# LayerNorm of a convolution branch, computed on token rows instead of by matmuls with a matrix of ones

## The chip, the cores and the metric

The kernel runs on one core of a Trainium2 chip. The metric is the device time of one execution in microseconds (us), as the median of several runs. The core has five engines that each run their own instruction list in order and wait for one another through semaphores: TensorE (PE, matmul; PEld is its weight load), VectorE (DVE), ScalarE (ACT), GpSimd (POOL) and SyncE (SP, which here issues the transfers).

## What is computed

The program is an encoder of two layers over 256 tokens of width 1024. Each layer is a SwiGLU block, a pair of mixers side by side (windowed attention and a convolution), a second SwiGLU block and a gated embedding. The change lies in the convolution mixer, and there in one step:

```python
def layer_norm(x, g, b, eps=1e-5):
    mu = jnp.mean(xf, axis=-1, keepdims=True)
    var = jnp.mean(jnp.square(xf - mu), axis=-1, keepdims=True)
    y = (xf - mu) * lax.rsqrt(var + eps)
    return y * g + b
...
c_val, c_gate = jnp.split(c, 2, axis=-1)
c = c_val * jax.nn.sigmoid(c_gate)
c = depthwise_conv(c, conv_w[i], conv_b[i])          # 31 taps
c = jax.nn.silu(layer_norm(c, conv_ln_g[i], conv_ln_b[i]))
y_conv = c @ w_conv_out[i]
g_attn, g_conv = jnp.split(jax.nn.sigmoid(g), 2, axis=-1)
h = h + (g_attn * y_attn + g_conv * y_conv) @ w_o[i]
```

The convolution has 512 channels, so for each of the 256 tokens a mean and a variance are taken over 512 values.

## The kernel before

Activations are kept with the channel on the 128 partitions and the token along the row: `y`, the convolution's result, is 128 x 4 x 256 (four groups of 128 channels, 256 tokens). Large weights are not used as they come. `Weights` loads a unit of 1 MB into one of four raw buffers (line 76, on SP's queue), ACT rounds it to a high part `w_hi` (line 100) and DVE forms the remainder `w_lo` (line 101); a product is then three matmuls, high x high, high x low and low x high (lines 311 to 313). A raw buffer is free for the next load once these two are through with it. The weights of the attention output and the convolution output are the exception: they are used as they are, in plain float32 (`raw_spec`, and `products` at line 847), and their buffers are free when the last matmul has read them.

The order of work on each engine is made by a scheduler that goes by priorities; products are put out in groups, and the evacuation of a group's PSUM tile is put out after the first product of the next one (`group`, `flush`). PSUM tiles of one bank (`mm_tile`) come from a pool of four.

In `mix`, the stage around the change runs so: the last gates are computed (`ps_g`); the attention output is formed in four groups, `attn_out` (tile `ps_ao`, line 847, 8 plain matmuls each), and between these groups stands the LayerNorm; then the convolution output in four groups (`conv_out`, tile `ps_co`, 32 plain matmuls), which multiplies by the gates and adds the attention's part (lines 908 and 909), and splits the sum into `ym_h` and `ym_l` (lines 444 and 445); then the output projection (`mix_out`, tile `ps_wo`), which needs both and the split weights w_o. The 31 taps of the convolution run on DVE (line 607) and end during the attention output.

The LayerNorm before has the channels on partitions, so a sum over channels is a sum over partitions, and it is taken on PE: `ln_mean` multiplies `y` by a 128 x 128 matrix of 1/512 (`ones_c`), which leaves the mean of each token in every partition (`ps_mu`, line 866). DVE subtracts it (line 868), ACT squares (line 871, `ysq`), `ln_scale` multiplies the squares by the same matrix (`ps_var`, line 876), ACT takes the root (line 364), DVE the reciprocal over 128 x 256 (line 366), DVE scales (line 880), and ACT applies gain, bias and Silu (line 881). `table` (line 379) has ACT load the table of Silu ahead of it.

Of the kernel before, what the change touches and what calls it, by code (L numbers as in the profile page):

```python
# [9 lines left out]
F32 = mybir.dt.float32  # L10
F32R = mybir.dt.float32r
AF = mybir.ActivationFunctionType
ALU = mybir.AluOpType
AX = mybir.AxisListType

P = 128
T = 256
# [7 lines left out]
CD = 512  # L25
KC = CD // P
# [112 lines left out]
def encoder_kernel(ctx: ExitStack, tc: tile.TileContext, a: dict, out: bass.AP):  # L139
    nc = tc.nc  # L140
    PS = bass.MemoryType.PSUM

    const = ctx.enter_context(tc.tile_pool(name="const", bufs=1))
# [3 lines left out]
    tmp = ctx.enter_context(tc.tile_pool(name="tmp", bufs=2))  # L147
# [4 lines left out]
    def mm_tile(name):  # L152
        return mmp.tile([P, 512], F32, name=name, tag="mm")
# [5 lines left out]
    ident = const.tile([P, P], F32, name="ident")  # L159
# [130 lines left out]

    ones_d = const.tile([P, P], F32, name="ones_d")
    nc.gpsimd.memset(ones_d, 1.0 / D)
    ones_c = const.tile([P, P], F32, name="ones_c")
    nc.gpsimd.memset(ones_c, 1.0 / CD)
    eps6 = const.tile([P, 1], F32, name="eps6")
    nc.gpsimd.memset(eps6, 1e-6)
    eps5 = const.tile([P, 1], F32, name="eps5")
    nc.gpsimd.memset(eps5, 1e-5)

    def pcol(name, l, k):  # L300
        c0, n = col[name]
        return par[:, c0 + l * n + k : c0 + l * n + k + 1]
# [59 lines left out]
    def rsqrt_of(ps, eps, name, **kw):  # L362
        sd = tmp.tile([P, T], F32, name="sd", bufs=1)
        nc.scalar.activation(out=sd, in_=ps, func=AF.Sqrt, bias=eps)
        r = tmp.tile([P, T], F32, name=name, **kw)
        nc.vector.reciprocal(out=r, in_=sd)
        return r
# [9 lines left out]
    def table(func):  # L377

        tc.keep_in_program_order(nc.scalar.preload_act_table(func))
# [59 lines left out]
    def bcast(r, n):  # L439
        return r.unsqueeze(1).broadcast_to([P, n, T])  # L440
# [9 lines left out]
    with tc.manual_schedule(engines={mybir.EngineType.Activation, mybir.EngineType.DVE}):  # L450
# [7 lines left out]
        for k in range(KD):  # L458
            xT[k] = (mm_tile if 2 <= k < 6 else at_tile)("ps_xt")[:, :T]
            for t in range(2):  # L460
# [5 lines left out]
                out=xl, in0=xT[k], scalar=gain, in1=xh.bitcast(F32), op0=ALU.mult, op1=ALU.subtract  # L466
# [122 lines left out]
    def mix(l, u, st, xn, stat):  # L589
        cw, kg, bias, sink = (late[n] for n in ("cw", "kg", "bias", "sink"))  # L590
        with tc.tile_pool(name="mix_pool", bufs=1) as mp:
# [3 lines left out]
            y = mp.tile([P, KC, T], F32, name="y")  # L595
# [236 lines left out]
            def squash(i):  # L832
                gs = g[:, i : i + 4, :]
                tc.keep_in_program_order(nc.scalar.activation(out=gs, in_=gs, func=AF.Sigmoid))
# [17 lines left out]
            def attn_out(f):  # L852
                ps = mm_tile("ps_ao")

                def evac():
                    gs = g[:, f : f + 2, :]
                    nc.vector.tensor_tensor(out=gs, in0=ps.rearrange("p (c t) -> p c t", c=2), in1=gs, op=ALU.mult)

                group([lambda: products(ps, o)], evac)

            ysq = mp.tile([P, KC, T], F32, name="ysq", tag="sqq")

            def ln_mean():
                ps = mm_tile("ps_mu")
                for i in range(KC):
                    nc.tensor.matmul(ps[:, :T], ones_c, y[:, i, :], start=i == 0, stop=i == KC - 1)
                for i in range(0, KC, 2):
                    nc.vector.tensor_tensor(
                        out=y[:, i : i + 2, :], in0=y[:, i : i + 2, :], in1=bcast(ps[:, :T], 2), op=ALU.subtract
                    )  # L870
                    nc.scalar.activation(out=ysq[:, i : i + 2, :], in_=y[:, i : i + 2, :], func=AF.Square)

            def ln_scale():
                ps = mm_tile("ps_var")
                for i in range(KC):
                    nc.tensor.matmul(ps[:, :T], ones_c, ysq[:, i, :], start=i == 0, stop=i == KC - 1)
                rs = rsqrt_of(ps[:, :T], eps5, "rs", bufs=1)
                table(AF.Silu)
                for i in range(KC):
                    nc.vector.tensor_tensor(out=y[:, i, :], in0=y[:, i, :], in1=rs, op=ALU.mult)  # L880
                    nc.scalar.activation(
                        out=y[:, i, :], in_=y[:, i, :], func=AF.Silu,
                        scale=pcol("conv_ln_g", l, i), bias=pcol("conv_ln_b", l, i),
                    )

            for i in range(KC):
                if i == 1:
                    ln_mean()
                if i == 2:
                    ln_scale()  # L890
                attn_out(2 * i)
                if i == 0:
                    squash(12)
# [126 lines left out]
    for l in range(L):  # L1020
        with tc.tile_pool(name="ffn1_pool", bufs=1) as hp:
            hooks = {1: lambda: late_loads(hp), 5: late_params, 6: lambda: late_tables(hp), 8: late_write, 12: late_bias} if l == 0 else {}
            xn, stat = new_x("xa", f"xm{l}"), Stat()
            ffn(hp, l, x_cur, st, "norm_mix", xn, stat, hooks)
        x_cur, st = xn, stat.finish(3, tokens=True)
        xn, stat = new_x("xa", f"xf{l}"), Stat()
        mix(l, x_cur, st, xn, stat)
        x_cur, st = xn, stat.finish(3)
        with tc.tile_pool(name="ffn2_pool", bufs=1) as hp:
            xe = (hp.tile([P, KD, T], F32R, name="xe_h"), hp.tile([P, KD, T], F32R, name="xe_l"))  # L1030
            stat = Stat()
            ffn(hp, l, x_cur, st, "norm_pe", xe, stat, {0: lambda: embed_load(l), 4: lambda: embed_input(hp)})
            x_cur, st = xe, stat.finish(4)
            xn, stat = (new_x("xa", f"xn{l}") if l + 1 < L else None), Stat()
            embed(l, x_cur, st, xn, stat)
            x_cur, st = xn, stat.finish(3)
# [39 lines left out]
```

## Time and profile before

| | |
|---|---|
| runs, us | 1176.48, 1177.25, 1177.78 (median 1177.25) |
| the profiled execution, us | 1176.52 |
| its span (first to last instruction), us | 1174.7 |
| granted TensorE clock, mean | 0.999 |
| busy: PE, DVE, ACT, POOL, us | 1156.8, 813.6, 614.2, 88.5 |
| HBM read, MB | 200.53 |

All times in the profile are from the span's start. PE's busy time counts matmuls that overlap in the pipeline, so the spacing from one to the next is read from rows that merge several: their length less the last one's duration, by their count less one. A row of the timeline is: start, length, engine, line, operation, output <- inputs, shape, count, and in brackets how long the engine had been idle and who ended that. A row of the groups is: line, engine, operation, tiles, shapes, count | busy us in all, mean ns of one | idle before. In rows of the waits three numbers follow: us in total, times, longest.

### The profile page before, as it was taken

To read this page: it belongs to the slowest core of one execution; us is meant where nothing else is said; L and a number is where in the kernel's file an instruction comes from. 1 tells how busy PE (TensorE), PEld (TensorE's weight loads), DVE (VectorE), ACT (ScalarE), POOL (GpSimd) and SP (SyncE) were. 2 spreads that over 40 slices of the span, in tenths; PEclk is the share of its full clock that TensorE was granted. 3 is DMA by queue.
4 is the path that set the end of the run, shared out by engine and by line. 5 is a ranking of instruction groups with operands and counts; after the bars stand their busy time and mean duration, and the time that the engine had idled before them with its cause. 6 is when DMAs were issued, how large, how long until landed. Compare 5 with 4: busy or idle time off the path is not lost.

```text
span 1174.7 us, 21809 instructions
## 1 busy us (share of the span) xinstructions
PE 1156.8 (98%) x9082; PEld 1121.5 (95%) x9082; DVE 813.6 (69%) x1214; ACT 614.2 (52%) x1033; POOL 88.5 (8%) x119
## 2 busy tenths in 40 slices
PE   7999999999999999999999999999999999999997
PEld 7999999998889999999999999999987999999997
DVE  5866656798667766656876666569976786666564
ACT  6644444676356544444664444457753564444443
POOL 3000001211002000001110000113000010000110
PEclk9999999999999999999999999999999999999999
DMA  8866556545074565556556464566522664654541
GB/s 252 265 229 209 167 178 200 179 147 141 2 249 161 189 200 175 171 165 214 188 166 204 156 205 152 170 213 193 145 72 68 219 224 159 201 168 144 192 144 37
DMA packets 195694, 202.99 MB, mean 173 GB/s; under 512 B 3731, under 2 KB 188899, under 8 KB 195596
## 3 DMA queue, kind: packets, MB, share of 16 engines
q1 hardware_dynamic: 195564, 201.60, 53.6%
q8 instruction: 71, 1.16, 0.4%
q14 instruction: 27, 0.22, 0.1%
q10 hardware_dynamic: 32, 0.01, 0.0%
HBM read 200.53 MB, written 1.06 MB: 172 GB/s over the span
## 4 chain that ended last, share of the span: by engine, by line
PE 96%; DVE 2%; DMA 1%; ACT 1%; issue 0%; SPq 0%; ACTq 0%
PE ps_gu L313 14%; PE ps_gu L311 14%; PE ps_gu L312 14%; PE ps_fo L313 7%; PE ps_fo L312 7%; PE ps_fo L311 7%; PE ps_g L311 3%; PE ps_g L313 3%; PE ps_g L312 3%; PE ps_co L847 2%; PE ps_s L755 1%; PE ps_c L311 1%; PE ps_pe L313 1%; PE ps_pe L312 1%; PE ps_pe L311 1%; PE ps_c L313 1%
## 5 line engine op out<-in xcount | busy, mean ns | idle before, releaser
L101 DVE TENSOR_TENSOR w_lo<-raw,w_hi 128x1024 fp32r<-128x1024 f32 (+1 forms) x368 | 440.9, 1202 | 241.5 <-ACT w_hi L100 237.4
L100 ACT CAST w_hi<-raw 128x1024 fp32r<-128x1024 f32 (+1 forms) x368 | 377.2, 1030 | 427.0 <-PE ps_gu L312 215.3
L313 PE MATMUL ps_fo<-h_hi,w_lo 128*128 128x256 f32 x704 | 198.6, 283 | 0.0
L312 PE MATMUL ps_fo<-h_lo,w_hi 128*128 128x256 f32 x704 | 198.6, 283 | 0.0
L311 PE MATMUL ps_fo<-h_hi,w_hi 128*128 128x256 f32 x704 | 198.6, 283 | 0.0
L313 PEld LDWEIGHTS ps_fo<-h_hi,w_lo 128*128 128x128 f32 x704 | 134.9, 192 | 0.0
L311 PEld LDWEIGHTS ps_fo<-h_hi,w_hi 128*128 128x128 f32 x704 | 134.9, 192 | 0.0
L312 PEld LDWEIGHTS ps_fo<-h_lo,w_hi 128*128 128x128 f32 x704 | 134.9, 192 | 0.0
L400 POOL TENSOR_TENSOR sq_acc<-sq_acc,sq 128x256 f32<-128x256 f32 x56 | 56.5, 1010 | 903.4 <-ACT sq L399 902.9
L311 PE MATMUL ps_gu<-x0h,w_hi 128*128 128x256 f32 x352 | 100.8, 286 | 2.1 <-ACT x L456 2.1
L607 DVE SCALAR_TENSOR_TENSOR y<-cpad,cw,y 128x256 f32<-128x256 f32 x240 | 101.1, 477 | 0.1
L313 PE MATMUL ps_gu<-x0h,w_lo 128*128 128x256 f32 x352 | 100.4, 285 | 0.2 <-DVE w_lo L101 0.2
L312 PE MATMUL ps_gu<-x0l,w_hi 128*128 128x256 f32 x352 | 100.2, 285 | 0.0
L311 PE MATMUL ps_gu<-xn0h,w_hi 128*128 128x256 f32 x352 | 99.8, 284 | 0.0
L312 PE MATMUL ps_gu<-xf0l,w_hi 128*128 128x256 f32 x352 | 99.8, 284 | 0.0
L312 PE MATMUL ps_gu<-xf1l,w_hi 128*128 128x256 f32 x352 | 99.8, 284 | 0.0
L311 PE MATMUL ps_gu<-xf0h,w_hi 128*128 128x256 f32 x352 | 99.7, 283 | 0.0
L311 PE MATMUL ps_gu<-xf1h,w_hi 128*128 128x256 f32 x352 | 99.7, 283 | 0.0
L313 PE MATMUL ps_gu<-xf0h,w_lo 128*128 128x256 f32 x352 | 99.6, 283 | 0.0
L313 PE MATMUL ps_gu<-xn0h,w_lo 128*128 128x256 f32 x352 | 99.6, 283 | 0.0
L312 PE MATMUL ps_gu<-xn0l,w_hi 128*128 128x256 f32 x352 | 99.6, 283 | 0.0
L313 PE MATMUL ps_gu<-xf1h,w_lo 128*128 128x256 f32 x352 | 99.6, 283 | 0.0
(222 smaller groups left out, 2718.6 us busy)
## 6 DMA issues: line engine op xcount, KB each, us to landing
raw<-in_w_ffn_in_dram SPq DMA_DIRECT2D x86, 1024.0 KB
raw<-in_w_in_dram SPq DMA_DIRECT2D x30, 1024.0 KB
raw<-in_w_ffn_out_dram SPq DMA_DIRECT2D x32, 896.0 KB
raw<-in_w_ffn_out_dram SPq DMA_DIRECT2D x16, 1024.0 KB
raw<-in_w_o_dram SPq DMA_DIRECT2D x8, 1024.0 KB
raw<-in_w_pe_gate_dram SPq DMA_DIRECT2D x8, 1024.0 KB
raw<-in_w_attn_out_dram SPq DMA_DIRECT2D x8, 512.0 KB
raw<-in_w_conv_out_dram SPq DMA_DIRECT2D x4, 1024.0 KB
```

What stands on the lines that cost most here:

```text
L100: nc.scalar.copy(out=hv[:, :, d0 : d0 + w], in_=src),
L101: nc.vector.tensor_tensor(out=lv[:, :, d0 : d0 + w], in0=src, in1=hv[:, :, d0 : d0 + w].bitcast(F32), op=ALU.subtract,),
L311: nc.tensor.matmul(ps, wh[:, k0 + k, cols], xh[:, kx, :], start=f, stop=False)
L312: nc.tensor.matmul(ps, wh[:, k0 + k, cols], xl[:, kx, :], start=False, stop=False)
L313: nc.tensor.matmul(ps, wl[:, k0 + k, cols], xh[:, kx, :], start=False, stop=e)
L400: nc.gpsimd.tensor_tensor(out=self.acc, in0=self.acc, in1=sq, op=ALU.add)
L607: nc.vector.scalar_tensor_tensor(out=y[:, i, :], in0=src, scalar=w, in1=y[:, i, :], op0=ALU.mult, op1=ALU.add)
L755: nc.tensor.matmul(ps[:, c, :], qT[v * HD : (v + 1) * HD, c, qb * P : (qb + 1) * P], kT[v * HD : (v + 1) * HD, :], start=True, stop=True,)
L847: nc.tensor.matmul(ps[:, c * T : (c + 1) * T], w[:, k, c * P : (c + 1) * P], x[:, k, :], start=k == 0, stop=k == KC - 1,)
```

## The change

The LayerNorm is computed with the token on the partition. `ln_by_token` transposes `y` on PE, 128 x 128 at a time, into two PSUM tiles `ps_yt` (one for each 128 tokens, with 512 channels along the row); DVE takes the statistics of each row with BN_STATS and BN_AGGR into `mv` (mean and variance of each token); ACT takes the root of the variances (128 x 2), DVE the reciprocal, and DVE writes the normalised rows to `yn`, one pass for each tile. `ln_by_channel` transposes `yn` back on PE into two tiles `ps_yc`, and ACT applies gain, bias and Silu out of PSUM into `y`. The matrix `ones_c` and its memset go. The first half stands where the mean stood (ahead of the second attention group), the second half ahead of the fourth group; before, the second half stood ahead of the third.

```diff
-    ones_c = const.tile([P, P], F32, name="ones_c")
-    nc.gpsimd.memset(ones_c, 1.0 / CD)
...
-            ysq = mp.tile([P, KC, T], F32, name="ysq", tag="sqq")
-            def ln_mean():
-                ps = mm_tile("ps_mu")
-                for i in range(KC):
-                    nc.tensor.matmul(ps[:, :T], ones_c, y[:, i, :], start=i == 0, stop=i == KC - 1)
+            yn = mp.tile([P, 2, CD], F32, name="yn", tag="sqq")
+            def ln_by_token():
+                mv = tmp.tile([P, 2, 2], F32, name="mv")
+                ps = []
+                for t in range(2):
+                    ps.append(mm_tile("ps_yt"))
+                    for i in range(KC):
+                        nc.tensor.transpose(ps[t][:, i * P : (i + 1) * P], y[:, i, t * P : (t + 1) * P], ident)
+                    six = tmp.tile([P, 6], F32, name="six")
+                    nc.vector.bn_stats(out=six, in_=ps[t])
+                    nc.vector.bn_aggr(out=mv[:, t, :], in_=six)
+                rs = tmp.tile([P, 2], F32, name="rs")
+                nc.scalar.activation(out=rs, in_=mv[:, :, 1], func=AF.Sqrt, bias=eps5)
+                nc.vector.reciprocal(out=rs, in_=rs)
+                table(AF.Silu)
+                for t in range(2):
+                    nc.vector.tensor_scalar(
+                        out=yn[:, t, :], in0=ps[t], scalar1=mv[:, t, 0:1], scalar2=rs[:, t : t + 1],
+                        op0=ALU.subtract, op1=ALU.mult,
+                    )
+            def ln_by_channel():
                 for i in range(0, KC, 2):
-                    nc.vector.tensor_tensor(
-                        out=y[:, i : i + 2, :], in0=y[:, i : i + 2, :], in1=bcast(ps[:, :T], 2), op=ALU.subtract
-                    )
-                    nc.scalar.activation(out=ysq[:, i : i + 2, :], in_=y[:, i : i + 2, :], func=AF.Square)
-            def ln_scale():
-                ps = mm_tile("ps_var")
-                for i in range(KC):
-                    nc.tensor.matmul(ps[:, :T], ones_c, ysq[:, i, :], start=i == 0, stop=i == KC - 1)
-                rs = rsqrt_of(ps[:, :T], eps5, "rs", bufs=1)
-                table(AF.Silu)
-                for i in range(KC):
-                    nc.vector.tensor_tensor(out=y[:, i, :], in0=y[:, i, :], in1=rs, op=ALU.mult)
-                    nc.scalar.activation(
-                        out=y[:, i, :], in_=y[:, i, :], func=AF.Silu,
-                        scale=pcol("conv_ln_g", l, i), bias=pcol("conv_ln_b", l, i),
-                    )
+                    ps = mm_tile("ps_yc").rearrange("p (f t) -> p f t", f=2)
+                    for f in range(2):
+                        for t in range(2):
+                            nc.tensor.transpose(
+                                ps[:, f, t * P : (t + 1) * P], yn[:, t, (i + f) * P : (i + f + 1) * P], ident
+                            )
+                    for f in range(2):
+                        nc.scalar.activation(
+                            out=y[:, i + f, :], in_=ps[:, f, :], func=AF.Silu,
+                            scale=pcol("conv_ln_g", l, i + f), bias=pcol("conv_ln_b", l, i + f),
+                        )
             for i in range(KC):
                 if i == 1:
-                    ln_mean()
-                if i == 2:
-                    ln_scale()
+                    ln_by_token()
+                if i == 3:
+                    ln_by_channel()
                 attn_out(2 * i)
```

The scheduler places the new instructions. On PE, in layer 0, from the first attention matmul to the first of the output projection, the order before is:

```order
L847 MATMUL ps_ao<-o,raw 128x256 x8
L866 MATMUL ps_mu<-y,ones_c 128x256 x2
L847 MATMUL ps_ao<-o,raw 128x256 x6
L866 MATMUL ps_mu<-y,ones_c 128x256
L847 MATMUL ps_ao<-o,raw 128x256 x2
L866 MATMUL ps_mu<-y,ones_c 128x256
L876 MATMUL ps_var<-ysq,ones_c 128x256 x2
L847 MATMUL ps_ao<-o,raw 128x256 x9
L876 MATMUL ps_var<-ysq,ones_c 128x256 x2
L847 MATMUL ps_ao<-o,raw 128x256 x7
L847 MATMUL ps_co<-y,raw 128x256 x32
L311 MATMUL ps_wo<-ym_h_3783,w_hi 128x256 x3
```

and in the changed kernel (its lines are 2 lower up to the LayerNorm and 9 higher behind it):

```order
L845 MATMUL ps_ao<-o,raw 128x256 x8
L867 MATMUL ps_yt<-ident,y 128x128 x4
L845 MATMUL ps_ao<-o,raw 128x256 x6
L867 MATMUL ps_yt<-ident,y 128x128 x2
L845 MATMUL ps_ao<-o,raw 128x256 x6
L867 MATMUL ps_yt<-ident,y 128x128 x2
L845 MATMUL ps_ao<-o,raw 128x256 x4
L886 MATMUL ps_yc<-ident,yn 128x128 x2
L845 MATMUL ps_ao<-o,raw 128x256 x8
L886 MATMUL ps_yc<-ident,yn 128x128 x6
L845 MATMUL ps_co<-y,raw 128x256 x32
L309 MATMUL ps_wo<-ym_h_3791,w_hi 128x256 x4
```

The sixteenth attention matmul, with which the first raw buffer comes free, had three mean matmuls ahead of it and now has six transposes. The first two transposes back stand ahead of the last eight attention matmuls, and the projection begins with four products of the high halves where it began with three.

On DVE, at the same place, from the last two taps to the first evacuation of the convolution output (`w_lo` is the split of the weights w_o), the order before is:

```order
L607 SCALAR_TENSOR_TENSOR y<-cpad,cw,y 128x256 x2
L857 TENSOR_TENSOR g<-ps_ao,g 128x512
L868 TENSOR_TENSOR y<-y,ps_mu 128x512 x2
L101 TENSOR_TENSOR w_lo<-raw,w_hi 128x1024 x2
L857 TENSOR_TENSOR g<-ps_ao,g 128x512
L366 RECIPROCAL rs<-sd 128x256
L880 TENSOR_TENSOR y<-y,rs 128x256 x4
L857 TENSOR_TENSOR g<-ps_ao,g 128x512
L101 TENSOR_TENSOR w_lo<-raw,w_hi 128x1024 x4
L908 TENSOR_TENSOR g<-ps_co,g 128x512
```

and in the changed kernel:

```order
L605 SCALAR_TENSOR_TENSOR y<-cpad,cw,y 128x256 x2
L855 TENSOR_TENSOR g<-ps_ao,g 128x512
L869 BN_STATS six<-ps_yt 128x6 x2
L870 BN_AGGR mv<-six 128x2 x2
L855 TENSOR_TENSOR g<-ps_ao,g 128x512
L873 RECIPROCAL rs<-rs 128x2
L876 TENSOR_SCALAR yn<-ps_yt,mv,rs 128x512 x2
L101 TENSOR_TENSOR w_lo<-raw,w_hi 128x1024 x2
L855 TENSOR_TENSOR g<-ps_ao,g 128x512
L101 TENSOR_TENSOR w_lo<-raw,w_hi 128x1024 x3
L917 TENSOR_TENSOR g<-ps_co,g 128x512
```

The first two splits, which stood ahead of the reciprocal, now stand behind the whole LayerNorm; and the third attention evacuation stands ahead of the small reciprocal.

On DVE again, from there to the first `ym_l`, which the projection waits for, before:

```order
L101 TENSOR_TENSOR w_lo<-raw,w_hi 128x1024 x4
L908 TENSOR_TENSOR g<-ps_co,g 128x512
L909 TENSOR_TENSOR g<-g 128x512
L101 TENSOR_TENSOR w_lo<-raw,w_hi 128x1024
L908 TENSOR_TENSOR g<-ps_co,g 128x512
L445 TENSOR_TENSOR ym_l_3784<-g,ym_h_3783 128x512
```

and in the changed kernel:

```order
L101 TENSOR_TENSOR w_lo<-raw,w_hi 128x1024 x3
L917 TENSOR_TENSOR g<-ps_co,g 128x512
L101 TENSOR_TENSOR w_lo<-raw,w_hi 128x1024
L918 TENSOR_TENSOR g<-g 128x512
L917 TENSOR_TENSOR g<-ps_co,g 128x512
L918 TENSOR_TENSOR g<-g 128x512
L917 TENSOR_TENSOR g<-ps_co,g 128x512
L101 TENSOR_TENSOR w_lo<-raw,w_hi 128x1024
L443 TENSOR_TENSOR ym_l_3792<-g,ym_h_3791 128x512
```

Two evacuations of the convolution output and two sums stand ahead of the fifth split where there was one of each, and none stands between that split and `ym_l`. The order of transfers on SP is the same in both kernels. On ACT the changed kernel rounds the weights w_o twice ahead of the four Silu and five times behind them. Layer 1 has the same order in each kernel.

## The prediction

> **What bounds the kernel now.** I read the page first, then the busy time by stretches, then who PE waited for, then the chain that ended last, and last the order of time around the projections behind the attention.
>
> ```profile
> span 1174.7 us, 21809 instructions
> PE 1156.8 (98%) x9082; PEld 1121.5 (95%) x9082; DVE 813.6 (69%) x1214; ACT 614.2 (52%) x1033; POOL 88.5 (8%) x119
> PE 96%; DVE 2%; DMA 1%; ACT 1%; issue 0%; SPq 0%; ACTq 0%
> ```
>
> PE is busy 98% of the span and is 96% of the chain that ended last. Time can only be won in two ways: less work on PE, or fewer of its few waits. The table by stretches shows where the LayerNorm stage lies in both layers, and that PE is not full there (columns: stretch, length, busy time of PE, PEld, DVE, ACT, POOL, granted clock, DMA).
>
> ```profile
> 313.50:334.00 20.50, 17.78 (x83) 15.01 (x82) 12.43 (x21) 8.00 (x10) 0.00 (x0) 1.00 0.27 88
> 334.00:348.00 14.00, 14.00 (x65) 12.35 (x66) 9.81 (x13) 6.95 (x9) 0.00 (x0) 1.00 0.88 287
> 889.60:910.00 20.40, 17.83 (x83) 15.06 (x82) 12.46 (x21) 8.03 (x10) 0.00 (x0) 1.00 0.29 91
> ```
>
> PE lacks 2.72 us in the first layer's stretch and 2.57 in the second's, at a full clock; the stretch behind it, 334 to 348, is full. The waits name the reason, and both are the LayerNorm's own:
>
> ```profile
> PE ps_var L876 <- ACT ysq L871: 3.2, 2, 1.6
> PE ps_co L847 <- ACT y L881: 2.1, 2, 1.1
> ```
>
> So per layer: 1.6 us for the squares ahead of the variance and 1.1 us for the first normalised channel ahead of the convolution output. The chain, in order of time, in layer 0:
>
> ```profile
> 313.71 3.46 PE ps_ao L847 x16
> 317.17 0.86 PE ps_mu L866 x4
> 321.95 5.09 DMA raw<-in_w_o_dram
> 327.06 1.05 ACT w_hi L100
> 328.14 2.36 DVE w_lo L101 x2
> 330.50 0.60 DVE g L857
> 331.10 1.67 DVE rs L366
> 333.31 0.61 ACT y L881
> 333.97 14.08 PE ps_co L847 x64
> ```
>
> A matmul of plain float32 shows as two records: 16 records in 3.46 us are 8 matmuls of 0.43 us. The reciprocal over 128x256 stands behind two splits of weights that had waited for a transfer.
>
> **The change, PE's work.** It takes away 8 matmuls per layer (four for the mean, four for the variance; 4 records take 0.86 us): 8 x 0.43 = 3.44 us. It adds 16 transposes. The trace has the same transposes, for the attention, eight in a row, and the duration of one by itself:
>
> ```profile
> 277.63 1.03 PE L792 MATMUL ps_pt<-ident,s 128*128 128x128 f32 x8
> L792 PE MATMUL ps_pt<-ident,s x64: 270/272/332, 272.6 to 877.6; 128*128 128x128 f32 x64
> ```
>
> Eight in 1.03 us with 0.27 for the last are (1.03 - 0.27) / 7 = 0.108 us from one to the next. 16 x 0.108 = 1.73 us, so PE's work falls by 1.71 us per layer.
>
> **The change, the chain that PE waits for.** What is added on DVE and ACT, by the nearest rows:
>
> ```profile
> L857 DVE TENSOR_TENSOR g<-ps_ao,g 128x512 f32<-128x512 f32 x8 | 5.5, 687 | 6.8 <-PE ps_ao L847 6.8
> L765 DVE CUSTOM_DVE_ANT_0 s<-ps_s,bias,sink 128x256 f32<-128x256 f32 x32 | 13.6, 479 | 5.9 <-PE ps_s L755 4.0 <-PE ps_pt L792 1.9
> L366 DVE RECIPROCAL rs<-sd 128x256 f32<-128x256 f32 x2 | 3.5, 1743 | 0.0
> L421 ACT ACTIVATE sd_tok<-ps_stat,eps x2: 255/256/257, 214.7 to 790.8; 128x4 f32<-128x4 f32 x2
> L423 DVE RECIPROCAL r_tok<-sd_tok x2: 120/120/120, 216.5 to 792.6; 128x4 f32<-128x4 f32 x2
> L379 ACT ACT_TABLE_LOAD x2 | 2.6, 1283 | 0.0
> L881 ACT ACTIVATE y<-y,par 128x256 f32<-128x256 f32 x8 | 4.4, 591 | 2.3 <-DVE y L880 2.3
> ```
>
> BN_STATS and BN_AGGR are in no row. From below: a pass over 512 elements out of PSUM takes 0.69 us (0.60 when the next follows). The dearest DVE operation per element is the reciprocal, 1743 / 256 = 6.8 ns, which for 512 would be 3.5 us. In between, a pass with a running reduction (L765) takes 479 ns for 256, no more than other passes of its size. BN_STATS is a streaming reduction, so I take 0.69 and keep 3.5 as the upper end. For BN_AGGR and the tiny reciprocal I take 0.13 (L423), for the root over 128x2 0.26 (L421), for the normalising pass 0.69. The root's table load runs early, as ACT is idle after the last sigmoid; the Silu table (1.28) is covered by the transposes.
>
> Now PE's row in the new order, from 313.71. Eight attention matmuls to 317.17, four transposes to 317.60, six matmuls to 320.20, two transposes to 320.42, two matmuls to 321.28, four to 323.01, the last two transposes to 323.23. Their input is there: the last taps of the convolution end before 319 (the row below). Then four matmuls to 324.96, and the first two transposes back must wait for the normalised row.
>
> ```profile
> 317.88 0.99 DVE L607 SCALAR_TENSOR_TENSOR y<-cpad,cw,y 128x256 f32<-128x256 f32 x2
> ```
>
> On DVE: two BN_STATS from 323.3 end at 324.6, two BN_AGGR at 324.9, the root on ACT at 325.2; the third attention group, which PE ends at 324.96, is evacuated first (the DVE order has it ahead of the reciprocal), to 325.85; reciprocal 326.0; first normalising pass 326.7. So PE stands from 324.96 to about 326.75: 1.8 us, with eight ready matmuls queued behind the wait. They follow to 330.43, six transposes to 331.08, and the first Silu (0.59) lets the convolution output start near 331.6 instead of 333.97, 2.35 earlier. As a sum: 1.71 less work, waits of 1.8 + 0.5 in place of 2.72; the 0.25 between 2.1 and 2.35 is in no row (313.71 + 13.84 + 3.44 + 2.72 also falls 0.26 short of 333.97). I take the step by step figure; the sum is within the range.
>
> **What is late next.** The output projection needs weights that come through the raw buffers, and its input's low half. These rows are that path:
>
> ```profile
> 330.53 0.37 SPq L76 DMA_DIRECT2D raw<-in_w_o_dram  x1
> 332.89 0.37 SPq L76 DMA_DIRECT2D raw<-in_w_o_dram  x1
> 335.59 1.99 ACT L100 CAST w_hi<-raw 128x1024 fp32r<-128x1024 f32 x2 [0.69 <-DMA raw<-in_w_o_dram]
> 336.66 2.36 DVE L101 TENSOR_TENSOR w_lo<-raw,w_hi 128x1024 fp32r<-128x1024 f32 x2 [1.84 <-ACT w_hi L100]
> 338.52 1.99 ACT L100 CAST w_hi<-raw 128x1024 fp32r<-128x1024 f32 x2 [0.44 <-DMA raw<-in_w_o_dram]
> 339.05 0.37 SPq L76 DMA_DIRECT2D raw<-in_w_o_dram  x1
> 343.96 1.04 ACT L100 CAST w_hi<-raw 128x1024 fp32r<-128x1024 f32 x1 [3.44 <-DMA raw<-in_w_o_dram]
> 344.91 0.61 ACT L444 CAST ym_h<-g 128x512 fp32r<-128x512 f32 x1
> 345.03 1.23 DVE L101 TENSOR_TENSOR w_lo<-raw,w_hi 128x1024 fp32r<-128x1024 f32 x1 [1.75 <-ACT w_hi L100]
> 346.78 0.68 DVE L445 TENSOR_TENSOR ym_l<-g,ym_h 128x512 fp32r<-128x512 f32 x1
> 348.23 0.28 PE L312 MATMUL ps_wo<-ym_l,w_hi 128*128 128x256 f32 x1
> ```
>
> Each transfer waits for a buffer: the first for the 16th attention matmul (321.95), the second for the splits of the first (330.50), the fourth for the splits of the second (339.02). ym_l ends at 347.46, and PE reaches it at 348.23: about 0.7 us of slack. This path doesn't move by 2.35. The 16th matmul comes 0.65 earlier, since six transposes (0.65) stand ahead of it in place of three mean matmuls (1.29); cast and splits follow as before (DVE is free at 327.4), so the second transfer's cast starts at 334.94 and the third's 2.93 later, at 337.87. From 339.0 DVE has a full queue in the new order: splits and gate passes of 1.13, 0.60, 1.13, 0.60, 0.60, 0.75, 0.60, 1.23 and ym_l with 0.69 end at 346.4. PE ends the convolution output at 331.6 + 13.84 = 345.44, does four products that need only the high half (0.12 each) to 345.9, and waits 0.6 for ym_l, until 346.5. That is 1.73 before 348.23, with one product (0.12) more behind it: **1.85 us per layer**. Behind that point the weights come earlier too (the SP queue's order is the same), and PE is full as before.
>
> **Sum.** Two layers (the second has the same rows and the same order): 3.7 us. The profiled execution took 1176.52, 1.8 over its span: 1172.8. The median of the runs, 1177.25, is 0.7 above that execution, so on it 1173.55, which I round to **1173.6**. The rest costs nothing: ones_c's memset ran on POOL at the start, where nothing waits for it, and yn takes the buffer of ysq.
>
> **Rivals.**
> *All of PE's gain is kept (0.11).* If the DVE queue from 339.0 is 0.6 shorter than I add up, ym_l is no wait: 2 x 2.35 = 4.7, 1172.5. Against it: every piece of that queue has a row.
> *The statistics cost more, in part (0.11).* Each us on the two BN_STATS together moves the normalised row, and nearly all of it shows, since PE and the splits both stand behind it. BN_STATS of 0.85 to 1.65 us gives 0 to 3.3 us of gain; at 1.2, 1.85 - 1.0 = 0.85 per layer, 1175.5.
> *The statistics turn it slower (0.07).* The point is 1.85 = 2 x (t - 0.69), t = 1.6 us for one BN_STATS. At the reciprocal's price of 3.5 each layer loses 2 x 2.8 - 1.85 = 3.8 us: 1184.8. For it: no row shows the instruction. Against it: row L765, a reduction at the price of a plain pass.
> *Transposes at their latency (0.04).* If each took the 272 ns of the single row, PE would do 16 x 0.164 = 2.6 us more and the start at 331.6 would become 334.2: 0.2 late per layer, 1177.7, no change. The row of eight in 1.03 us speaks against it. The Trainium skill, "TensorE: Matmul & The Clock Gate", Part 4: PE-mode transpose, gives about 275 ns for a transpose in a kernel, says that latency dominates it and that transposes don't count as busy for the clock. By it this change would save nothing; the trace agrees with the duration of one and not with its use as a spacing, and it shows a granted clock of 1.00 in the stretch.
> *The second and third weight transfers share the way (0.07).* They are issued 0.6 us apart now, not 2.36. If they shared it evenly, the second would land some 2.2 later, ym_l would end near 348.5, and each layer would lose about 0.9: 1179. Against it: 330.53 to 335.59 is 5.06 us with the third in flight for the last 2.7, while the first alone took 5.11 (321.95 to 327.06).
>
> **How the numbers follow.** A measurement of this kernel can tell about 0.2%, 2.35 us, from no change. My forecast has 0.60 (waits and hand-overs 0.4 off per layer either way). Faster by over 0.2%: 0.60 + 0.11 + 0.03 of the dearer statistics (below 1.0 us each) = 0.74. Slower by over 0.2%: 0.07 for the statistics and 0.02 of the shared way = 0.09. The rest, 0.17, is no change. The range: below to 1172.0, the full gain and 0.5; above to 1176.9, which takes in the dearer statistics nearly to their turning point; outside are about 2 in 10.
>
> **What would show it.** ps_yt and ps_yc transposes 0.11 us apart; PE idle for yn about 1.8 us and for y about 0.5; ps_co starting 2.35 earlier; a wait of 0.6 for ym_l ahead of ps_wo where there was none; BN_STATS near 0.69. I am wrong if BN_STATS takes over 1 us, if the wait for ym_l is absent or over 1.5 us, or if stretches far from this stage move.

## The result and the profile after

The changed kernel takes 1158.15 us (median of 4 runs, 1156.98 to 1158.72) against 1177.3 beside it: a ratio of 0.9837, interval 0.982 to 0.9854. That is 19 us, where 3.7 were forecast; the direction was right, and the time lies far outside the range. The page begins (span, busy times, the chain that ended last):

```profile
span 1155.2 us, 21808 instructions
PE 1137.2 (98%) x9082; PEld 1102.3 (95%) x9082; DVE 811.0 (70%) x1214; ACT 610.9 (53%) x1029; POOL 87.4 (8%) x118
PE 95%; DMA 3%; DVE 1%; ACT 1%; issue 0%; SPq 0%; ACTq 0%; DVEq 0%
```

PE has as many records as before (9082; in each layer 8 float32 matmuls, which are 16 records, went, and 16 transposes came) and is busy 19.6 us less, when the change alone takes some 3.4 of work off it. So first the stage itself. The stretches of the attention output and of the convolution output (columns as in the prediction's table):

```profile
309.80:328.00 18.20, 16.01 (x83) 13.60 (x82) 12.27 (x22) 6.56 (x8) 0.00 (x0) 1.00 0.20 63
328.00:342.20 14.20, 14.10 (x65) 12.10 (x65) 8.39 (x10) 6.95 (x10) 0.00 (x0) 1.00 0.90 290
```

Rows of PE's timeline there in layer 0 (those between them are left out), and then of DVE's:

```profile
309.87 3.62 PE L845 MATMUL ps_ao<-o,raw 128*128 128x256 f32 x16
313.32 0.60 PE L867 MATMUL ps_yt<-ident,y 128*128 128x128 f32 x4
323.13 0.41 PE L886 MATMUL ps_yc<-ident,yn 128*128 128x128 f32 x2 [1.86 <-DVE yn L876]
327.98 14.08 PE L845 MATMUL ps_co<-y,raw 128*128 128x256 f32 x64 [0.33 <-ACT y L890]
342.16 0.74 PE L309 MATMUL ps_wo<-ym_h,w_hi 128*128 128x256 f32 x4
343.50 0.39 PE L310 MATMUL ps_wo<-ym_l,w_hi 128*128 128x256 f32 x1 [0.60 <-DVE ym_l L443]
```

```profile
319.47 1.30 DVE L869 BATCH_NORM_STATS2 six<-ps_yt 128x6 f32<-128x512 f32 x2 [1.15 <-PE ps_yt L867]
320.68 0.30 DVE L870 BATCH_NORM_AGGREGATE mv<-six 128x2 f32<-128x6 f32 x2
322.18 1.53 DVE L876 TENSOR_SCALAR yn<-ps_yt,mv,rs 128x512 f32<-128x512 f32 x2
...
340.20 0.68 DVE L917 TENSOR_TENSOR g<-ps_co,g 128x512 f32<-128x512 f32 x1
341.62 1.23 DVE L101 TENSOR_TENSOR w_lo<-raw,w_hi 128x1024 fp32r<-128x1024 f32 x1 [0.74 <-ACT w_hi L100]
342.76 0.68 DVE L443 TENSOR_TENSOR ym_l<-g,ym_h 128x512 fp32r<-128x512 f32 x1
```

The stage does what was forecast. From the first attention matmul to ps_co it takes 18.11 us (309.87 to 327.98) where it took 20.42 (from the row below, of the kernel before, to 333.97): 2.31 earlier, forecast 2.35.

```profile
313.55 3.62 PE L847 MATMUL ps_ao<-o,raw 128*128 128x256 f32 x16
```

But its start already lies 3.7 us earlier in the span, ahead of any LayerNorm. What runs ahead of it is the first SwiGLU, in which the change touches nothing. The next rows count the matmuls in stretches of 48 us inside the SwiGLU stages. Each matmul lasts 0.28 us and overlaps the next, so the spacing is 48.28 us by the count. First the kernel before, then the changed one (stretch, length, busy time and count of PE, granted clock, DMA share, GB/s); 80 to 128 and 430 to 478 lie in the first product, ps_gu, of layer 0's two SwiGLU blocks, 150 to 198 and 496 to 544 in their second, ps_fo (which in the kernel before begins at 498.2):

```profile
80.00:128.00 48.00, 48.00 (x403) 1.00 0.66 219
150.00:198.00 48.00, 48.00 (x402) 1.00 0.57 187
430.00:478.00 48.00, 48.00 (x402) 1.00 0.53 173
496.00:544.00 48.00, 48.00 (x402) 1.00 0.54 180
```

```profile
80.00:128.00 48.00, 48.00 (x402) 1.00 0.66 220
150.00:198.00 48.00, 48.00 (x426) 1.00 0.64 204
430.00:478.00 48.00, 48.00 (x402) 1.00 0.57 184
496.00:544.00 48.00, 48.00 (x426) 1.00 0.59 195
```

From the start of one product to the start of the next, ps_gu stays at 120.1 ns; ps_fo goes from 120.1 to 113.3, at a granted clock of 1.00 in both, with the same instructions in the same order and no wait. (These are by the count, good to 0.3 ns. The 528 products of a whole ps_fo start from 141.76 to 205.00 before, 120.0 ns apart, and from 141.62 to 201.37 after, 113.4 ns apart.) The group of ps_fo, before and after (one of three lines that read alike):

```profile
L311 PE MATMUL ps_fo<-h_hi,w_hi 128*128 128x256 f32 x704 | 198.6, 283 | 0.0
```

```profile
L309 PE MATMUL ps_fo<-h_hi,w_hi 128*128 128x256 f32 x704 | 193.7, 276 | 0.0
L309 PE MATMUL ps_pp<-pT_h,w_hi 128*128 128x256 f32 x32 | 8.8, 276 | 0.0
```

ps_pe and ps_pp, the products of the gated embedding, are faster too (ps_pp had a mean of 283 before). 3 x 704 products of ps_fo, 384 of ps_pe and 96 of ps_pp, each some 6.7 ns sooner, would be 2592 x 6.7 = 17.4 us. The last five of the eight groups of 24 that make up ps_pe in layer 1 gain less: there one product starts at 1139.80 and the eighteenth after it at 1141.92, which is 117.8 ns apart. That takes 120 x 4.5 = 0.5 us off, and 16.9 are left. The rest of the 19.5 us between the two profiled executions (1176.52 and 1156.98), 2.6, would be the LayerNorm's.

**What moved.** SBUF is the memory on the chip that the engines read their operands from; a tile lies at one address in each of its 128 partitions. `ones_c` was 512 bytes of each SBUF partition, and `rs`, 128x256, was 1024; the new small tiles take 192 in its place. In the built programs everything behind them slid down: the split weights by 512 bytes, x (behind them, ahead of the pool `tmp`) by 512, and h, xe and pT (behind `tmp`) by 512 + 832 = 1344. So x kept its distance from the weights, and h did not. (The moving operand of a matmul is the one that is sent through the weights loaded ahead of it: 256 columns of x or h here. A distance modulo 256 is what is left of it when whole multiples of 256 bytes are taken off.)

| operand | address before, after | distance from w_hi, modulo 256 | spacing, ns |
|---|---|---|---|
| w_hi, w_lo | 65184, 64672 (w_lo 28672 further) | | |
| x, moving in ps_gu | 130720, 130208 | 0, 0 | 120.1, 120.1 |
| h, moving in ps_fo | 162720, 161376 | 0, 192 | 120.1, 113.3 |

**Theory P** (place): a product's spacing depends on where its moving operand lies against the split weights in the partition; the change made its 17 us by chance, by moving h. **Theory L** (LayerNorm): the gain comes from the new order or the shorter stage, by way of what runs beside PE. For P the same gain must come without the LayerNorm, and go with it.

### The profile page after: what moved, and what is told of

Its sections match the earlier page's. It is cut to its first block, busy times and chain, and to the rows that moved or that the text cites. A ratio compares the mean times of both kernels' runs of the same rounds, so it can differ in the third digit from the quotient of the medians.

```text
span 1155.2 us, 21808 instructions
## 1 busy us (share of the span) xinstructions
PE 1137.2 (98%) x9082; PEld 1102.3 (95%) x9082; DVE 811.0 (70%) x1214; ACT 610.9 (53%) x1029; POOL 87.4 (8%) x118
## 4 chain that ended last, share of the span: by engine, by line
PE 95%; DMA 3%; DVE 1%; ACT 1%; issue 0%; SPq 0%; ACTq 0%; DVEq 0%
PE ps_gu L311 15%; PE ps_gu L309 15%; PE ps_gu L310 15%; PE ps_fo L311 7%; PE ps_fo L310 7%; PE ps_fo L309 7%; PE ps_g L309 3%; PE ps_g L311 3%; PE ps_g L310 3%; DMA raw<-in_w_o_dram 2%; PE ps_ao L845 2%; PE ps_s L753 1%; PE ps_wo L310 1%; PE ps_c L309 1%; PE ps_c L311 1%; PE ps_c L310 1%
## 5 line engine op out<-in xcount | busy, mean ns | idle before, releaser
L309 PE MATMUL ps_fo<-h_hi,w_hi 128*128 128x256 f32 x704 | 193.7, 276 | 0.0
L310 PE MATMUL ps_fo<-h_lo,w_hi 128*128 128x256 f32 x704 | 193.7, 276 | 0.0
L311 PE MATMUL ps_fo<-h_hi,w_lo 128*128 128x256 f32 x704 | 193.7, 276 | 0.0
L309 PEld LDWEIGHTS ps_fo<-h_hi,w_hi 128*128 128x128 f32 x704 | 131.9, 188 | 0.0
L310 PEld LDWEIGHTS ps_fo<-h_lo,w_hi 128*128 128x128 f32 x704 | 131.8, 188 | 0.0
L311 PEld LDWEIGHTS ps_fo<-h_hi,w_lo 128*128 128x128 f32 x704 | 131.8, 188 | 0.0
```

Source lines behind the costliest of these rows:

```text
L309: nc.tensor.matmul(ps, wh[:, k0 + k, cols], xh[:, kx, :], start=f, stop=False)
L310: nc.tensor.matmul(ps, wh[:, k0 + k, cols], xl[:, kx, :], start=False, stop=False)
L311: nc.tensor.matmul(ps, wl[:, k0 + k, cols], xh[:, kx, :], start=False, stop=e)
```

## The experiments

All edits put unused room into a pool (a tile that POOL clears at the start and nobody reads) or turn a single order. Each batch ran beside the kernel before, which took 1176.4 to 1176.9 us in them.

**e1, the old LayerNorm with h moved.** To the kernel before:

```
+    pad_t = tmp.tile([P, 48], F32, name="pad_t", bufs=1)
+    nc.gpsimd.memset(pad_t, 0.0)
```

> The kernel before, with its old LayerNorm, and one unused tile of 192 bytes per partition in the pool tmp, which moves the tiles of the SwiGLU pools (h_hi, h_lo, xe, pT) by 192 bytes and nothing that lies ahead of them. Their distance from the weight tiles, modulo 512 bytes, becomes what it is in the changed kernel (448 in place of 256). If the spacing of these matmuls hangs on where their moving operand lies (by itself or against the weights): ps_fo and ps_pe at 113.4 ns instead of 120, 4 x 3.5 + 2 x 1.3 + 0.6 = 17.2 us less, about 1160 us. If it is the new LayerNorm that speeds them up: 120 ns, 1177 us.

1160.26 us, ratio 0.9864 (0.9849 to 0.9879). The kernel before, with 192 bytes that nobody uses, is 16.7 us faster, close to the 16.9 of the products:

```profile
80.00:128.00 48.00, 48.00 (x403) 1.00 0.67 219
150.00:198.00 48.00, 48.00 (x426) 1.00 0.61 197
```

**e2, the new LayerNorm with h put back.** To the changed kernel: the same two lines with 80 elements, 320 bytes, which brings h to 0 modulo 256 again.

> The changed kernel with one unused tile of 320 bytes per partition in tmp, which brings the SwiGLU tiles back to the distance from the weights that they have in the kernel before (256 modulo 512). If the place of the tiles gives the speed: ps_fo and ps_pe at 120 ns again, and what is left is the LayerNorm's own gain, which I put at 3.7 us in the prediction: 1173.6 us (1175.5 if the output projection keeps more of it back). If the new LayerNorm itself gives it: 113.4 ns and 1158 us.

1174.97 us, ratio 0.9984 (0.9975 to 0.9993): 1.95 us under the kernel before. ps_fo is at 120 again (x403 below), and the stage is as in the changed kernel. Theory L falls. PE in layer 0, and the first products behind the stage (shortest, mean and longest ns, first start and last end):

```profile
150.00:198.00 48.00, 48.00 (x403) 1.00 0.57 187
```

```profile
314.21 3.62 PE L848 MATMUL ps_ao<-o,raw 128*128 128x256 f32 x16
332.33 14.08 PE L848 MATMUL ps_co<-y,raw 128*128 128x256 f32 x64 [0.33 <-ACT y L893]
346.59 0.74 PE L312 MATMUL ps_wo<-ym_h,w_hi 128*128 128x256 f32 x4 [0.18 <-ACT ym_h L445]
347.93 0.38 PE L313 MATMUL ps_wo<-ym_l,w_hi 128*128 128x256 f32 x1 [0.60 <-DVE ym_l L446]
```

```profile
L312 PE MATMUL ps_gu<-xf0h,w_hi x5: 280/283/283, 370.3 to 371.7; 128*128 128x256 f32 x5
```

18.12 us up to ps_co is 2.30 better than before. From ps_co to the next SwiGLU it takes 38.0, where the kernel before takes 36.6:

```profile
L311 PE MATMUL ps_gu<-xf0h,w_hi x4: 281/283/283, 370.6 to 371.7; 128*128 128x256 f32 x4
```

So 1.3 of the 2.3 us are given back behind ps_co; e9 asks where.

**e3, all moved together.** To the kernel before, a tile of 48 elements in the pool of constants, ahead of the raw buffers and all behind them.

> The kernel before with 192 unused bytes per partition ahead of all tiles, so that weights, x, h and all others move together. If the place of the moving operand by itself decides: h lies modulo 512 as in e1, so ps_fo at 113.4 ns, and ps_gu too since x moves as h does: 1177 - 17 - 28 or less, at most 1160 us. If its distance from the weights decides: no change, 120 ns everywhere and 1177 us.

1176.76 us, ratio 0.9996 (0.9986 to 1.0006), x402 and x403 in the stretches. The place as such does nothing.

**e12, weights, x and h moved against what is ahead of them.** To the kernel before, a pool of 48 elements between the raw buffers and the weights.

> The kernel before with 192 bytes of room between the raw buffers and the split weights: w, x and h move together by 192 against the raw buffers, the constants and the tiles ahead of them. If the distance of the moving operand from the weights decides: as before, 1176.9 within 1, all at 120 ns. If it were the distance from the raw buffers or the constants (with whose traffic the reads might collide): ps_fo or ps_gu at another spacing and 1135 to 1165.

1176.54 us, ratio 0.9999 (0.9989 to 1.0009), x402 in all four stretches. With e1 and e3 this leaves only distances between the weights and what lies behind them. A rival that was not tried by a run, the traffic of the other engines on the weights, is answered by the trace of the kernel before: where DVE, ACT and POOL stand and hardly a transfer runs, 19 products of ps_g, which read x at a distance of 0, are still 2.28 / 19 = 0.120 us apart (columns: PE, PEld, DVE, ACT, POOL, clock, DMA share, GB/s):

```profile
311.40:313.40 2.00, 2.00 (x19) 2.00 (x18) 0.00 (x0) 0.00 (x0) 0.00 (x0) 1.00 0.03 8
```

**e4, x moved as well.** To the kernel before, a pool of 48 elements between the weights and x, which moves x and h.

```
+    padp = ctx.enter_context(tc.tile_pool(name="padp", bufs=1))
     xp = ctx.enter_context(tc.tile_pool(name="xp", bufs=1))
...
+    pad_x = padp.tile([P, 48], F32, name="pad_x")
+    nc.gpsimd.memset(pad_x, 0.0)
```

> The kernel before with 192 unused bytes per partition between the pool of weights and the pool of x, so that x and the SwiGLU tiles both lie 192 bytes further from the weights (192 and 448 modulo 512). If the distance from the weights decides, and 192 is as good as 448: the 4224 matmuls of ps_gu and those of ps_c and ps_g (1152) go to about 113.4 ns as well, 5376 x 6.6 ns = 35 us on top of e1's 17: about 1125 us, if PE stays the bound. If only h's own place matters: ps_gu stays at 120 and the time is e1's, 1160. If the LayerNorm is the cause: 1177.

1135.04 us (1130.14 to 1135.45), ratio 0.9634 (0.9618 to 0.965): 42 us under the kernel before, on the old LayerNorm, yet 10 short of what was expected. x and h kept their distance from one another here, so that one is not what counts. The same distance of 192 modulo 256 gives two spacings in one execution: 113.3 ns at the start of the first SwiGLU, 117.8 in the rest of it, from 53 us on, and 113.3 in the three others.

```profile
26.00:41.00 15.00, 15.00 (x135) 1.00 0.68 213
80.00:128.00 48.00, 48.00 (x410) 1.00 0.66 215
150.00:198.00 48.00, 48.00 (x410) 1.00 0.64 204
430.00:478.00 48.00, 48.00 (x426) 1.00 0.53 174
496.00:544.00 48.00, 48.00 (x426) 1.00 0.68 222
```

Of the 10 us that are missing, 5.7 are this first SwiGLU (worked out under e5). ps_c and ps_g, the products of x ahead of the attention, have both spacings in both layers, with a mean of 116 to 117, which is another 3.4 by the trace. In none of the fourteen traces does the spacing change within an unbroken row of 60 or more such products of one tile; at one distance it changes where other instructions of PE stand between them.

**e5, the new LayerNorm with both.** To the changed kernel, e4's pool and 80 elements in `tmp`.

> The changed kernel with 192 bytes of unused room between the weights and x, and 320 bytes in the small pool: x lies 192 bytes from the weights modulo 512 and h 448, as in the run e4, but with the new LayerNorm. Placement theory: the LayerNorm's own 1.95 us come on top of e4's 1135.0, so 1133.1, and ps_gu is 113 to 118 ns apart. If what e4 left at 118 ns in layer 0 was a matter of chance in that execution, some runs are near 1127 (all of ps_gu at 113.3). If the LayerNorm alone had made the gain (its theory), 1158 as the changed kernel.

1128.08 us, ratio 0.9596 (0.9576 to 0.9615), in two groups: 1127.38, 1127.61, 1128.08 and 1133.54, 1133.71. The profiled one is of the slower group and has e4's counts. The first SwiGLU from 53 us on has 739 products of ps_gu and 528 of ps_fo; 4.5 ns on each would be 5.7 us, about the distance between the groups. That the faster runs have 113.3 ns there too is therefore likely, but no profile of one shows it.

**e6, e7, e8, e10: other distances.** To the changed kernel, the pool of e4 with 16, 80, 8 and 56 elements, and 32 in `tmp` for the first three. The two guesses at a rule, A and B, are told in the first expectation below.

> The changed kernel with other room: x lies 64 bytes from the weights modulo 512, h 128. Theory A, only multiples of 256 bytes are slow: all products with split weights near 113.3 ns, 1126 to 1133 us. Theory B, the spacing falls evenly from 120 ns at a multiple of 256 to 113.3 at 64 or more bytes short of it and is in between for less: ps_gu near 115 to 118, ps_fo at 113 to 116, some 1140 to 1155. LayerNorm theory: 1158.

> The changed kernel with x 320 bytes and h 384 bytes from the weights modulo 512, which is e6's 64 and 128 with 256 more. If the distance counts modulo 256, the same time and the same spacings as e6 within 3 us. If it counts modulo 512 alone, another time. Theory A: 1126 to 1133. LayerNorm theory: 1158.

> The changed kernel with x 32 bytes and h 96 bytes from the weights modulo 512. Theory A, only multiples of 256 are slow: 1126 to 1133, as in e6. Theory B, graded: ps_gu at 117 to 120 ns, ps_fo at 114 to 118, some 1150 to 1168. LayerNorm theory: 1158.

> The changed kernel with x 224 bytes from the weights modulo 256 and h 160 (modulo 512: 224 and 160). If the fast place is a band around 192, ps_gu and ps_fo at 113.3 ns: 1126 to 1133. If 192 is a single fast place among others, ps_gu and ps_fo at 116 to 120 as at 32, 64, 96 and 128: 1155 to 1175.

They took 1160.83 (0.9865, 0.9847 to 0.9883), 1160.32 (0.986, 0.9842 to 0.9878), 1159.03 (0.9849, 0.9831 to 0.9867) and 1162.05 us (0.9877, 0.9859 to 0.9895). The ps_gu and ps_fo stretches of e6, e8 and e10:

```profile
80.00:128.00 48.00, 48.00 (x410) 1.00 0.67 221
150.00:198.00 48.00, 48.00 (x407) 1.00 0.61 194
```

```profile
80.00:128.00 48.00, 48.00 (x414) 1.00 0.65 219
150.00:198.00 48.00, 48.00 (x402) 1.00 0.61 198
```

```profile
80.00:128.00 48.00, 48.00 (x408) 1.00 0.67 224
150.00:198.00 48.00, 48.00 (x411) 1.00 0.58 190
```

e7 has e6's counts, 410 and 407, so at these two distances it counts modulo 256. Both guesses at a rule fall: A, since only one of the places tried is at 113.3, and B, since 96 bytes are as slow as 0.

| distance modulo 256 | 0 | 32 | 64 | 96 | 128 | 160 | 192 | 224 |
|---|---|---|---|---|---|---|---|---|
| ns from product to product | 120.1 | 116.6 | 117.8 | 120.1 | 118.6 | 117.5 or 118.6 | 113.3 or 117.8 | 118.3 |

These are from the first SwiGLU, of x for 32, 64 and 224, of h for 96, 128 and 160, and of both for 0 and 192; each of the six between was tried with one of the two alone. Of these four kernels one changes its pace within the run: e10's third ps_fo stage counts 407, not 411, which is 118.6 ns. An operand that no experiment was made for agrees with the table: `ym`, moving in ps_wo, lies at 224 in the kernel before, where ps_wo's spacing is 118.3, and at 160 in the changed kernel, where it is 118.7 in layer 0 and 117.3 in layer 1.

**e9, where the LayerNorm's other half went.** In the changed kernel DVE stands 0.74 us for a cast and then splits a slice of w_o for 1.14 us, just ahead of `ym_l` (the last rows of DVE above). PE reads that slice, the seventh of eight, only after six others. One line keeps its cast and split in program order, behind the gates and `ym_l`; all addresses are those of the changed kernel:

```
             ws.lag = 0
+            ws.pin = tc.keep_in_program_order
             mix_out(0, 2)
```

> The changed kernel as it is (same places in SBUF), with one edit: the rounding and split of the seventh slice of w_o, which PE needs only some 17 us later, is kept behind the gate passes and ym_l on ACT and DVE. Theory of the fourth transfer: DVE stood 0.74 us idle for that slice's cast and then split it for 1.14 us ahead of ym_l, so the waits between ps_co and the next SwiGLU (37.93 and 37.12 us against 36.63 before) go; 1.3 + 0.5 = 1.8 us, 1156.3, with no wait for ym_l in the list. Rival, that ym_l is late for another reason (the gate passes themselves): no change, 1158.1 within 0.5.

1155.57 us, ratio 0.9825 (0.9812 to 0.9839): 21.1 under the kernel before, where the changed kernel was 19.2 under it, so 1.9. In the list of PE's waits the changed kernel has a row for `ym_l`, the first below. It is gone now; the LayerNorm's two others, for `yn` and `y`, are as they were:

```profile
PE ps_wo L310 <- DVE ym_l L443: 1.0, 2, 0.6
PE ps_yc L886 <- DVE yn L876: 3.7, 2, 1.9
PE ps_co L845 <- ACT y L890: 0.7, 2, 0.3
```

and PE goes from ps_co (328.29) through ps_wo to the next SwiGLU without a gap, in 36.4 us:

```profile
328.29 14.08 PE L845 MATMUL ps_co<-y,raw 128*128 128x256 f32 x64 [0.33 <-ACT y L890]
342.02 0.70 PE L309 MATMUL ps_wo<-ym_h,w_hi 128*128 128x256 f32 x3
342.56 0.28 PE L310 MATMUL ps_wo<-ym_l,w_hi 128*128 128x256 f32 x1
```

```profile
L309 PE MATMUL ps_gu<-xf0h,w_hi x7: 279/282/283, 364.7 to 366.9; 128*128 128x256 f32 x7
```

In the changed kernel this took 37.9. Of the 1.5 us, 0.3 are ps_wo's spacing, 117.3 here against 118.7; in layer 1 it is the other way round, so the 1.9 do not rest on it. The theory of the fourth transfer holds, and the rival falls.

**e11, all together.** e5's room and e9's line.

> The edits of e5 (room, so that x and h lie 192 modulo 256 from the weights) and of e9 (the seventh slice kept behind ym_l) together. If they add up: e5's two times, 1127.5 and 1133.6, each less 1.8: 1125.7 or 1131.8. If the split's order is of no account: as e5.

1130.72 us, ratio 0.9605 (0.9587 to 0.9623), from runs of 1126.1, 1130.52, 1130.92 and 1132.5. Its lowest is 1.3 under e5's lowest, and the other three 1 to 3 under e5's upper group, which fits edits that add up, as well as one run in the faster group can show it. Its median is above e5's only because three of its four runs fell into the slower group, against two of five. Group by group it is the fastest version tried; its median is 4% under the kernel before and 2.4% under the changed one.

## Why the prediction was wrong

**The step that failed** is the last of the sum, "The rest costs nothing: ones_c's memset ran on POOL at the start, where nothing waits for it, and yn takes the buffer of ysq." It priced the instruction that goes and not the room in SBUF that goes with it, 512 bytes of `ones_c` and 832 of the small pool. The room moved h against the weights, which made nearly all of 2592 products 6.7 ns shorter: 16.9 us by the profile, 16.7 by e1. "PE is full as before" failed in the same way: PE was full, but not at the same pace. The sign that the prediction named, "if stretches far from this stage move", is what came. None of the rivals held this case.

**What held.** The transposes are 0.11 us apart ((0.60 - 0.27) / 3), so the rival of latency falls, and with it, as a price from one transpose to the next, the figure of about 275 ns that the Trainium skill, "TensorE: Matmul & The Clock Gate", Part 4, gives for a transpose in one kernel. Two BN_STATS take 1.30 together, what two of the nearest pass were taken for (0.69, and 0.60 where the next follows), not 3.5 each. The two waits of PE are 1.86 and 0.33 (forecast 1.8 and 0.5), and ps_co starts 2.31 earlier in layer 0 and 2.15 in layer 1 (2.35).

**What held in kind and not in size.** Behind ps_co the forecast gave back 0.5 us of a layer's 2.35, and the runs gave back 1.3 and 0.9 (layers 0 and 1 of e2), so that the LayerNorm by itself is worth 1.95 us there (0.8 to 2.9 by the interval) and not 3.7. In the changed kernel they gave back 1.3 and 0.5 (37.9 and 37.1 us where the kernel before takes 36.6 in both layers), so 2.7 are left there by these rows (2.31 + 2.15 - 1.3 - 0.5), near the 2.6 above. The forecast summed DVE's queue as if it never stood. It stood 0.74 for the cast of the fourth transfer of w_o. The row of ym_l's wait, 0.60, agrees with the forecast's 0.6 by luck: PE read ym_l 15.5 us behind the start of ps_co (327.98 to 343.50), where the forecast had 14.9 (331.6 to 346.5), for the four products ahead of it were late too (in e2 PE stood 0.18 for `ym_h`).

```profile
340.54 1.05 ACT L100 CAST w_hi<-raw 128x1024 fp32r<-128x1024 f32 x1 [4.23 <-DMA raw<-in_w_o_dram]
```

In the changed kernel that cast, the row above, starts 5.73 us after the splits that free its buffer end (334.81); before, the two are 4.94 apart (339.02 and 343.96). The next load, of the SwiGLU's weights, is issued 1.7 us behind those splits now and was 3.0 behind them before, so that it shares more of the way. That the sharing makes the difference fits the rows, but was not tried by itself. ACT had the same cast ahead of `ym_h`, which the forecast left out. A rival named the sharing of the way, for the second and third transfer; it was the fourth. e9 shows that none of it had to be waited for.

## What to carry to other kernels

A tile that is added, removed or resized moves every tile behind it, and here that was worth six to nine times the edit itself (16.9 us against 2.6 or 1.95). Before a gain or a loss is put down to an edit, compare the addresses and the spacing of untouched matmuls far from it, and undo the move with unused room. What an engine does for a reader far ahead (here a split needed after six other slices) should not stand in its queue ahead of what is needed next.

## What the runs showed of the hardware

The spacing of matmuls of 128x128 by 128x256 (fp32r operands) with a new weight tile each varies from 113.3 to 120.1 ns with the distance of the moving operand from the weights in the partition, modulo 256 bytes, at a granted clock of 1.00. It doesn't depend on the place itself (e3, e12), and at a distance of 0 it is 0.120 us with the other engines idle too. The Trainium skill, "TensorE: Matmul & The Clock Gate", Part 2, gives PE two independent SBUF read ports, one for the streaming operand and one for the weights, so that loading the next tile's weights takes no bandwidth from the running matmul. Taken to mean that the two reads can't hinder one another at all, that would leave the distance without effect. The runs show an effect, for these shapes at least; whether it arises at the ports or behind them they don't show.

At two of the distances two spacings occur: 113.3 and 117.8 at 192, and 117.5 and 118.6 at 160. Each is steady as long as such products follow one another without a break. Which one it is can change where other instructions of PE stand between them (e4, at 53 us and from the first SwiGLU to the second; the changed kernel, within ps_pe of layer 1) and, by the times, from run to run (e5). What sets it, and why of the eight distances only 192 was seen at 113.3, stays open: the two reads meeting in the same part of the memory would fit a distance modulo 256, but no run here shows what they meet in.
